# Split modulation weights in the first stage of a one-layer diffusion kernel

## The chip, the cores and the metric

The kernel runs on one core of a Trainium2 chip. It computes one layer of a hybrid diffusion backbone in float32. The metric is the device time of one execution in microseconds. Three runs of the kernel before gave 1940.58, 1941.0 and 1943.64 us, with a median of 1941.0.

The core has a matrix engine (TensorE, PE in the profile; its weight loads are shown apart as PEld), three engines for elementwise work (VectorE as DVE, ScalarE as ACT, GpSimd as POOL), and SyncE (SP), from whose queue the loads and stores are issued.

## The reference, cut to what matters

The layer modulates its normalised input with a shift and a scale that come from a conditioning vector. There are two such vectors: `c` for the latent tokens and `c_ctx` for the context tokens. The change touches the first two of six modulation parts only.

```python
mod = jax.nn.silu(c) @ w_mod[l] + b_mod[l]                       # (1, 6*1024)
mod_c = jax.nn.silu(c_ctx)[None, :] @ w_mod[l] + b_mod[l]
sh1, sc1, g1, sh2, sc2, g2 = jnp.split(mod, 6, axis=-1)
sh1c, sc1c, g1c, sh2c, sc2c, g2c = jnp.split(mod_c, 6, axis=-1)
h = modulate(rms_norm(x, norm1_w[l]), sh1, sc1)                  # latents, 1024 tokens
hc = modulate(rms_norm(ctx, norm1_w[l]), sh1c, sc1c)             # context, 256 tokens
```

with `modulate(h, shift, scale) = h * (1 + scale) + shift`. Everything after it (an input projection, attention over a window and the context, a chunked recurrence in two directions, a merge, a gated feed-forward part) is the same in both kernels.

## The kernel before

Arrays of 1024 channels are held as eight tiles of 128 partitions, and `KT` is 8. Most large products are made from split operands: a float32 value is written as a high part rounded to the type `F32R` and a low part, the rest, also in that type. TensorE multiplies such operands in one pass. Three products (high by high, high by low, low by high) stand in for one of full float32 precision; that is `mm3` at L86 to L93. The helper `split_from` (L47 to L49) makes a split: ACT copies the source into the high part (L44), and DVE subtracts the high part from the source into the low part (L49).

The first stage is `stage_startup` (L273 on). It loads the vectors, turns them on TensorE into `vecT` (L289, L290), and applies silu to both conditioning vectors, which gives `sil`, 128 partitions by 8 tiles by 2 vectors (L292). Then come two halves `i`, each with eight tiles `k` of modulation weights of 128 x 1024 floats, 512 KB each (L357 to L365). For each tile there are two products of 512 columns (L363). They are plain float32, the stationary operand is `sil[:, k]` with its two columns, and they accumulate into the two banks `pm[i]`. Of the sums only two rows are used, one for each vector. `modulation(i)` copies these rows out of both banks, one by DVE (L322) and one by ACT, turns them by eight transposes against an identity (`pmT`, L326) so that channels lie on partitions, and makes shift and scale from them with six small DVE operations (L330 to L332, tile `mods`). After the first half, the two context blocks are normalised (`norm`, L305 to L313), turned (`xct`, L348) and modulated for the first four channel tiles (`hfc` at L337 on ACT, then a split into `hcH` and `hcL`). After the second half the other four follow.

Weight tiles, token blocks and the raw context weights share one pool of eleven buffers of 128 x 1024 (`block`, tag `x`). A load into a buffer waits until the reader of what was in it is done. The loads are issued from SP's queue in program order. Split weights of the whole stage are kept in the pools of `Weights` (L53), with five buffers for high and five for low parts.

After the modulation, the stage makes the context keys (`pkc`) and values (`pvc`), the other context projections (`cx`), and the modulated latents (`xt`, `hf`, `hH`, `hL`), interleaved. The order on each engine is made by a list scheduler when the program is built, from the order in the source and its own estimates. Where `issue_after` is given, an operation is held behind another one. Each engine runs its own list strictly in order, apart from weight loads on TensorE.

Of the kernel before, what the change touches and what calls it, by code (L numbers as in the profile page):

```python
# [8 lines left out]
F32 = mybir.dt.float32  # L9
F32R = mybir.dt.float32r  # L10
AF = mybir.ActivationFunctionType
ALU = mybir.AluOpType
# [4 lines left out]
P = 128  # L17
D = 1024
# [3 lines left out]
KT = D // P  # L22
# [11 lines left out]
NFC = DFF // P  # L34
EPS = 1e-6
NEG = -1e30


class Ctx:
# [3 lines left out]
def copy_act(nc, out, in_, scale=1.0):  # L43
    return nc.scalar.activation(out, in_, AF.Copy, scale=scale)  # L44


def split_from(nc, hi, lo, src, eng="v"):  # L47
    h = copy_act(nc, hi, src)
    (nc.vector if eng == "v" else nc.gpsimd).tensor_tensor(lo, src, hi.bitcast(F32), op=ALU.subtract)  # L49
    return h  # L50
# [222 lines left out]
def stage_startup(E, at):  # L273
    nc, tc, A, ident, expo, vecT, mods = E.nc, E.tc, E.A, E.ident, E.expo, E.vecT, E.mods
    mm_tile, tp_tile, s_tile, wts = E.mm_tile, E.tp_tile, E.s_tile, E.wts
    H = KT // 2
    with ExitStack() as st:
        sp = st.enter_context(tc.tile_pool(name="st1", bufs=1, reuse_waits="tile"))
        wp = st.enter_context(tc.tile_pool(name="stw", bufs=2, reuse_waits="tile"))
        xp = st.enter_context(tc.tile_pool(name="stx", bufs=11, reuse_waits="tile"))  # L280

        def block(name):
            return xp.tile([P, D], F32, tag="x", name=name)
# [4 lines left out]
        for a in range(2):  # L288
            nc.tensor.transpose(pv[:, a * P : (a + 1) * P], rows[:, a], ident)  # L289
        nc.vector.tensor_copy(vecT, pv[:, :256])  # L290
        sil = E.sil3
        nc.scalar.activation(  # L292
            sil.rearrange("p k c -> p c k"), vecT[:, 0:16].rearrange("p (c k) -> p c k", c=2), AF.Silu
        )

        ss = sp.tile([P, NBLK], F32, name="ss")
        rs = sp.tile([P, NBLK], F32, name="rs")
# [5 lines left out]
            return t  # L303

        def norm(i, t, late=None):  # L305
            junk = wp.tile([P, D], F32, tag="junk", name=f"xj{i}", bufs=1)
            with ExitStack() as pin:
                if late is not None:
                    pin.enter_context(tc.issue_after(late.ins))
                nc.scalar.activation(junk, t, AF.Square, accum_out=ss[:, i : i + 1])  # L310
            nc.gpsimd.tensor_scalar(ss[:, i : i + 1], ss[:, i : i + 1], 1.0 / D, EPS, op0=ALU.mult, op1=ALU.add)
# [5 lines left out]
        pm = [[pm0[:2, 0:512], pm0[:2, 512:1024]], [mm_tile("pm2")[:2], mm_tile("pm3")[:2]]]  # L317
        bT = vecT[:, 32:48].rearrange("p (s k) -> p s k", s=2)

        def modulation(i):  # L320
            mrow = sp.tile([P, 1024], F32, name=f"mrow{i}", tag="mrow")[:2]
            nc.vector.tensor_copy(mrow[:, 0:512], pm[i][0])  # L322
            copy_act(nc, mrow[:, 512:1024], pm[i][1])
            pT = tp_tile(f"pmT{i}")
            for j in range(8):
                nc.tensor.transpose(pT[:, 2 * j : 2 * j + 2], mrow[:, j * P : (j + 1) * P], ident[:2, :2])  # L326
            pTv = pT[:, :16].rearrange("p (s k c) -> p s c k", s=2, c=2)
            ks = slice(H * i, H * i + H)
            for c in (1, 0):
                nc.vector.tensor_tensor(mods[:, 2 + c, ks], pTv[:, 0, c], bT[:, 0, ks], op=ALU.add)  # L330
                nc.vector.scalar_tensor_tensor(mods[:, c, ks], pTv[:, 1, c], 1.0, bT[:, 1, ks], op0=ALU.add, op1=ALU.add)
                nc.vector.tensor_tensor(mods[:, c, ks], mods[:, c, ks], vecT[:, 16 + H * i : 16 + H * i + H], op=ALU.mult)  # L332
# [25 lines left out]
        for i in range(2):  # L358
            for k in range(KT):
                w = block(f"wm{i}_{k}")  # L360
                nc.sync.dma_start(w, A["w_modA"][i][:, k])
                for n in range(2):
                    nc.tensor.matmul(  # L363
                        pm[i][n], sil[:, k], w[:, n * 512 : (n + 1) * 512], start=k == 0, stop=k == KT - 1
                    )  # L365
# [12 lines left out]
        for k2 in (2, 3):  # L378
            context(k2, pts[k2 - 2])

# [78 lines left out]
        for i in range(4):  # L459
# [222 lines left out]
def stage_mlstm(E, st):  # L682
# [96 lines left out]
    def gate_math():  # L779
        with ExitStack() as s2:  # L780
# [1068 lines left out]
def host_arrays(inp):  # L1849
# [81 lines left out]
```

## Time and profile before

| what | value |
|---|---|
| runs | 1940.58, 1941.0, 1943.64 us; median 1941.0 |
| profiled execution | span 1937.4 us from the first to the last instruction; its own time isn't given apart from the span |
| TensorE busy | 1903.1 us, 98% of the span |
| VectorE, ScalarE, GpSimd busy | 1442.4, 1000.5, 332.0 us |
| both modulation products in the chain | 15.57 us from 5.81 and 13.82 us from 23.22 |
| second half's modulated context starts | 39.21 us |

All times in the profile are microseconds from the span's start, in one execution. The chain that ended last is followed back from the last instruction, at each step to what released it. In a timeline row the first number is the start, the second the time taken, and the bracket at the end is the idle time of that engine before it and what ended it. In a group by form, the numbers are the busy time and the mean of one in ns, and then the idle time before.

### The profile page before, as it was taken

How to read it: one execution, taken by the hardware profiler on the slowest of the kernel's cores; microseconds unless marked ns; L12 is line 12 of the kernel's file. 1: busy time of each engine (PE TensorE's matmuls, PEld its weight loads, DVE VectorE, ACT ScalarE, POOL GpSimd, SP SyncE). 2: the span in 40 equal slices, each digit the busy share in tenths (PEclk: the TensorE clock that was granted, in tenths of full speed). 3: DMA queues.
4: the chain of work that ended last, by engine and by line, in shares of the span. 5: the costliest groups of instructions: out<-in, count | busy, mean ns of one | idle time of the engine just before them, and what ended most of it. 6: DMA issues, size and time to landing. Idle time of an engine off the chain costs nothing.

```text
span 1937.4 us, 28767 instructions
## 1 busy us (share of the span) xinstructions
PE 1903.1 (98%) x10012; PEld 1631.2 (84%) x10012; DVE 1442.4 (74%) x2886; ACT 1000.5 (52%) x1979; POOL 332.0 (17%) x534
## 2 busy tenths in 40 slices
PE   8999999999999999999999999999999999999999
PEld 3998888888888889999999888788888888888887
DVE  2867878777777666666657878669989898897564
ACT  4845656555556445353536556256545444455441
POOL 1323433433333132131311012010000000000000
PEclk9999999999999999999999999999999999999999
DMA  8731222313222323425235982722354534499841
GB/s 320 231 126 51 80 66 67 95 42 102 60 67 77 125 89 104 144 94 192 88 106 210 376 300 89 279 94 77 141 199 182 195 152 177 160 327 341 307 165 65
DMA packets 139377, 298.53 MB, mean 154 GB/s; under 512 B 15440, under 2 KB 39648, under 8 KB 136416
## 3 DMA queue, kind: packets, MB, share of 16 engines
q1 hardware_dynamic: 124832, 270.48, 40.3%
q10 hardware_dynamic: 14400, 26.22, 4.0%
q8 instruction: 78, 1.28, 0.3%
q14 instruction: 67, 0.55, 0.1%
HBM read 220.55 MB, written 76.10 MB: 153 GB/s over the span
## 4 chain that ended last, share of the span: by engine, by line
PE 83%; DVE 5%; DMA 4%; ACT 4%; issue 2%; POOL 1%; POOLq 0%; ACTq 0%; SPq 0%; DVEq 0%
PE pa L1513 4%; PE pa L1515 4%; PE pa L1514 4%; PE pt L625 3%; PE g L93 3%; PE g L92 3%; PE g L91 3%; PE yb L1515 2%; PE yb L1514 2%; PE yb L1513 2%; PE dx L1515 2%; PE dx L1513 2%; PE dx L1514 2%; PE pb L1513 2%; PE pb L1515 2%
## 5 line engine op out<-in xcount | busy, mean ns | idle before, releaser
L606 POOL TENSOR_SCALAR P<-P,st 128x640 f32<-128x640 f32 (+1 forms) x128 | 115.1, 916 | 261.0 <-DVE st L604 178.3
L597 ACT ACTIVATE P<-P,st 128x640 f32<-128x640 f32 (+1 forms) x128 | 102.6, 801 | 24.6 <-DVE st L593 24.0
L593 DVE CUSTOM_DVE_ANT_0 P<-s,maskA,nsink 128x640 f32<-128x640 f32 (+1 forms) x112 | 103.2, 921 | 9.4 <-PE s L590 7.8
L49 DVE TENSOR_TENSOR pl<-pt,ph 128x512 fp32r<-128x512 f32 x152 | 100.8, 686 | 10.1 <-ACT ph L44 8.6
L44 ACT ACTIVATE ph<-pt 128x512 fp32r<-128x512 f32 x152 | 87.4, 597 | 36.9 <-PE pt L625 32.5
L91 PE MATMUL g<-hH,fh 128*128 128x512 f32 x256 | 102.7, 401 | 0.0
L93 PE MATMUL g<-hH,fl 128*128 128x512 f32 x256 | 100.6, 393 | 0.0
L92 PE MATMUL g<-hL,fh 128*128 128x512 f32 x256 | 100.6, 393 | 0.0
L625 PE MATMUL pt<-ident,P 128*128 128x128 f32 x608 | 92.3, 273 | 3.5 <-POOL P L606 3.1
L91 PE MATMUL pq<-w1h,hH 128*128 128x384 f32 (+1 forms) x256 | 87.1, 340 | 0.2 <-DVE t L545 0.2
L91 PE MATMUL kv<-w1h,hH 128*128 128x384 f32 x256 | 86.5, 339 | 0.8 <-ACT w1h L44 0.8
L93 PE MATMUL pq<-w1h,hL 128*128 128x384 f32 (+1 forms) x256 | 86.7, 339 | 0.0
L92 PE MATMUL kv<-w1l,hH 128*128 128x384 f32 x256 | 86.6, 338 | 0.0
L92 PE MATMUL pq<-w1l,hH 128*128 128x384 f32 (+1 forms) x256 | 86.5, 338 | 0.0
L93 PE MATMUL kv<-w1h,hL 128*128 128x384 f32 x256 | 86.3, 337 | 0.0
L625 PEld LDWEIGHTS pt<-ident,P 128*128 128x128 f32 x608 | 71.1, 140 | 11.5 <-POOL P L606 6.4
L91 PE MATMUL mo<-w1h,hH 128*128 128x256 f32 x256 | 72.6, 284 | 0.4 <-ACT sg L774 0.2
L93 PE MATMUL mo<-w1h,hL 128*128 128x256 f32 x256 | 72.1, 282 | 0.0
L92 PE MATMUL mo<-w1l,hH 128*128 128x256 f32 x256 | 71.9, 281 | 0.0
L1651 ACT ACTIVATE cv<-ua,vecT 128x1024 f32<-128x1024 f32 x22 | 27.4, 1245 | 83.6 <-DVE ua L1624 83.6
L929 POOL TENSOR_SCALAR kwh<-k,gcall 128x128 fp32r<-128x128 f32 x72 | 32.7, 457 | 215.8 <-PE dC L92 112.1
L1513 PE MATMUL dx<-dwh,dfh 128*128 128x512 f32 x176 | 68.7, 390 | 0.0
(587 smaller groups left out, 6392.9 us busy)
## 6 DMA issues: line engine op xcount, KB each, us to landing
ur<-in_w_up SPq DMA_DIRECT2D x22, 1024.0 KB, 4.9
wmb<-in_w_modB SPq DMA_DIRECT2D x48, 256.0 KB, 2.9
f_d<-cv SPq DMA_DIRECT2D x22, 512.0 KB, 2.6
wm<-in_w_modA SPq DMA_DIRECT2D x16, 512.0 KB, 9.2
fr<-in_w_g SPq DMA_DIRECT2D x32, 256.0 KB, 3.1
drf<-fs_d SPq DMA_DIRECT2D x15, 512.0 KB, 6.8
drw<-wt_d SPq DMA_DIRECT2D x14, 512.0 KB, 6.0
w1b<-in_w_cx SPq DMA_DIRECT2D x16, 388.0 KB, 4.0
```

The source lines that it names most:

```text
L44: return nc.scalar.activation(out, in_, AF.Copy, scale=scale)
L49: (nc.vector if eng == "v" else nc.gpsimd).tensor_tensor(lo, src, hi.bitcast(F32), op=ALU.subtract)
L91: nc.tensor.matmul(ps, lh[:, ls], rh[:, rs], start=start and i == 0, stop=False)
L92: nc.tensor.matmul(ps, lh[:, ls], rl[:, rs], start=False, stop=False)
L93: nc.tensor.matmul(ps, ll[:, ls], rh[:, rs], start=False, stop=stop and i == n - 1)
L593: nc.vector.tensor_tensor_reduce(pm[:, :W], ps[:, off : off + W], mask[:, :W], scale=ss[:, h : h + 1], scalar=nsink[:, hh : hh + 1], op0=A ...
L597: nc.scalar.activation(pm[:, :W], pm[:, :W], AF.Exp, bias=st4[:, h : h + 1], scale=-1.0, accum_out=st4[:, 4 + h : 5 + h])
L606: nc.gpsimd.tensor_scalar(Ps[h][:, :W], Ps[h][:, :W], st4[:, 12 + h : 13 + h], 1.0, op0=ALU.mult, op1=ALU.mult)
L625: nc.tensor.transpose(pt[:, h * P : (h + 1) * P], Ps[h][:, kb * P : (kb + 1) * P], ident)
L1513: nc.tensor.matmul(ps, lh, rh, start=start and i == 0, stop=False, skip_group_check=True)
L1514: nc.tensor.matmul(ps, lh, rl, start=False, stop=False, skip_group_check=True)
L1515: nc.tensor.matmul(ps, ll, rh, start=False, stop=stop and i == n - 1, skip_group_check=True)
```

## The change

Of the eight weight tiles of each half, six (all but tiles 2 and 5, `WHOLE`) are now split into a high and a low part with `split_from`, into a pool of their own with two buffers for each part. The stationary operand for these is a new constant `sp4`: for each tile 100 columns (`MS`), of which columns 0 and 1 hold the high parts of the two vectors, columns 2 and 3 their low parts, and the rest zeros. So a product with the high and one with the low part of the weights, each for two banks, gives four rows: rows 0 and 1 belong to the high parts of the vectors and rows 2 and 3 to the low ones. They are made in one pass each, and with four partial products, where `mm3` has three. Tiles 2 and 5 keep the plain float32 products into rows 0 and 1 of the same banks.

The four rows must be added in pairs. This is done in the turning: the eight transposes are replaced by eight float32 products of the four rows with a 4 x 2 matrix `sel` of ones and zeros, which adds row 0 to row 2 and row 1 to row 3.

`sp4` takes one of the five high buffers of `Weights` until the second half's products are done. The pool `stw` of the later part of the stage is opened only after `modulation(1)`, in the place of the split tiles, and the tile `junk` of `norm` moves to another pool for it.

```diff
+MS = 100
+WHOLE = (2, 5)
@@ stage_startup
-        wp = st.enter_context(tc.tile_pool(name="stw", bufs=2, reuse_waits="tile"))
         xp = st.enter_context(tc.tile_pool(name="stx", bufs=11, reuse_waits="tile"))
+        sm = ExitStack()
+        md = sm.enter_context(tc.tile_pool(name="stm", bufs=2, reuse_waits="tile"))
...
+        sp4 = wts.hp.tile([P, 2, 400], F32R, tag="h", name="sp4").rearrange("p a b -> p (a b)").rearrange("p (k m) -> p k m", m=MS)
+        nc.gpsimd.memset(sp4.bitcast(F32), 0.0)
+        copy_act(nc, sp4[:, :, 0:2], sil)
+        nc.vector.tensor_tensor(sp4[:, :, 2:4], sil, sp4[:, :, 0:2].bitcast(F32), op=ALU.subtract)
+        sel = sp.tile([P, 2], F32, name="sel")
+        nc.vector.tensor_tensor(sel[:4], ident[:4, 0:2], ident[:4, 2:4], op=ALU.add)
...
-            mrow = sp.tile([P, 1024], F32, name=f"mrow{i}", tag="mrow")[:2]
-            nc.vector.tensor_copy(mrow[:, 0:512], pm[i][0])
-            copy_act(nc, mrow[:, 512:1024], pm[i][1])
+            mrow = sp.tile([P, 1024], F32, name=f"mrow{i}", tag="mrow")[:4]
+            nc.vector.tensor_copy(mrow[:, 0:512], pm[i][0][:4])
+            copy_act(nc, mrow[:, 512:1024], pm[i][1][:4])
             pT = tp_tile(f"pmT{i}")
             for j in range(8):
-                nc.tensor.transpose(pT[:, 2 * j : 2 * j + 2], mrow[:, j * P : (j + 1) * P], ident[:2, :2])
+                nc.tensor.matmul(pT[:, 2 * j : 2 * j + 2], mrow[:, j * P : (j + 1) * P], sel[:4], start=True, stop=True)
...
-                for n in range(2):
-                    nc.tensor.matmul(
-                        pm[i][n], sil[:, k], w[:, n * 512 : (n + 1) * 512], start=k == 0, stop=k == KT - 1
-                    )
+                if k in WHOLE:
+                    for n in range(2):
+                        nc.tensor.matmul(
+                            pm[i][n][:2], sil[:, k], w[:, n * 512 : (n + 1) * 512], start=False, stop=False,
+                            skip_group_check=True,
+                        )
+                else:
+                    wh, wl = [md.tile([P, D], F32R, tag=f"m{x}", name=f"m{x}{i}_{k}") for x in "hl"]
+                    split_from(nc, wh, wl, w)
+                    for x, wx in enumerate((wh, wl)):
+                        for n in range(2):
+                            nc.tensor.matmul(
+                                pm[i][n][:MS], sp4[:, k], wx[:, n * 512 : (n + 1) * 512], start=k == 0 and x == 0,
+                                stop=k == KT - 1 and x == 1, skip_group_check=True,
+                            )
...
         modulation(1)
+        sm.close()
+        wp = st.enter_context(tc.tile_pool(name="stw", bufs=2, reuse_waits="tile"))
```

In the order as built, the new work is placed as follows. On ACT the copies of the second half's tiles 0 and 1 stand before the first context work (`hfc`, `hcH`), those of tiles 3, 4, 6 and 7 behind it. On TensorE five of the second half's products, on tiles 0 and 1, stand ahead of the first half's turning. On DVE the subtraction of the second half's tile 0 stands ahead of the first half's row copy, and a subtraction of the context key weights stands between the first and the second of the six small operations of the second half's modulation. The rest of the program has the same order in both, but for a few neighbours that change places.

More of the change, by code (lines that the diff above doesn't have):

```diff
@@ L305, in norm @@
         def norm(i, t, late=None):
-            junk = wp.tile([P, D], F32, tag="junk", name=f"xj{i}", bufs=1)
+            junk = sp.tile([P, D], F32, tag="junk", name=f"xj{i}", bufs=1)
             with ExitStack() as pin:
@@ L316, in stage_startup @@
         pm0 = s_tile("pm0")
-        pm = [[pm0[:2, 0:512], pm0[:2, 512:1024]], [mm_tile("pm2")[:2], mm_tile("pm3")[:2]]]
+        pm = [[pm0[:, 0:512], pm0[:, 512:1024]], [mm_tile("pm2"), mm_tile("pm3")]]
         bT = vecT[:, 32:48].rearrange("p (s k) -> p s k", s=2)
         def modulation(i):
-            mrow = sp.tile([P, 1024], F32, name=f"mrow{i}", tag="mrow")[:2]
-            nc.vector.tensor_copy(mrow[:, 0:512], pm[i][0])
-            copy_act(nc, mrow[:, 512:1024], pm[i][1])
+            mrow = sp.tile([P, 1024], F32, name=f"mrow{i}", tag="mrow")[:4]
+            nc.vector.tensor_copy(mrow[:, 0:512], pm[i][0][:4])
+            copy_act(nc, mrow[:, 512:1024], pm[i][1][:4])
             pT = tp_tile(f"pmT{i}")
             for j in range(8):
-                nc.tensor.transpose(pT[:, 2 * j : 2 * j + 2], mrow[:, j * P : (j + 1) * P], ident[:2, :2])
+                nc.tensor.matmul(pT[:, 2 * j : 2 * j + 2], mrow[:, j * P : (j + 1) * P], sel[:4], start=True, stop=True)
             pTv = pT[:, :16].rearrange("p (s k c) -> p s c k", s=2, c=2)
```

## The prediction

> **What bounds the kernel now.** I read the page's first part, then the chain that ended last in order of time for the first 72 us, then the timeline of each engine there.
>
> ```profile
> span 1937.4 us, 28767 instructions
> PE 1903.1 (98%) x10012; PEld 1631.2 (84%) x10012; DVE 1442.4 (74%) x2886; ACT 1000.5 (52%) x1979; POOL 332.0 (17%) x534
> ```
>
> TensorE is busy for 98% of the span. The change lies in the first 2% of it, so what matters is how early the later work can start. The chain of the first stage:
>
> ```profile
> 1.64 4.04 DMA wm<-in_w_modA
> 5.81 15.57 PE pm L363 x32
> 23.22 13.82 PE pm L363 x32
> 37.05 1.02 PE xct L348 x8
> 38.07 0.59 PE pmT L326 x8
> 39.21 1.02 ACT hfc L337 x2
> 42.36 1.05 ACT xj L310 x2
> 49.76 2.22 ACT w1h L44 x3
> 63.57 0.67 ACT hf L337
> ```
>
> The two halves of the modulation product (pm) fill the chain up to 37 us; after the turning (pmT) the chain passes to ScalarE (ACT), which holds most of it past 63 us. So the handle on the end is the start of the second half's modulated context, hfc at 39.21: what follows it stands in the same order in both programs as built (a few neighbours swap), and I let a shift of hfc reach the end one for one.
>
> The loads, from the rows of the weight tiles' line (issue times, then the time to landing) and the stretch view (PE, PEld, DVE, ACT, POOL, clock, DMA share, GB/s):
>
> ```profile
> L361 SPq DMA_DIRECT2D wm<-in_w_modA x1: 327/327/327, 9.6 to 9.6; - x1
> DMA to landing us min/median/max: 10.3/10.3/10.3
> ...
> L361 SPq DMA_DIRECT2D wm<-in_w_modA x1: 328/328/328, 18.0 to 18.0; - x1
> DMA to landing us min/median/max: 8.3/8.3/8.3
> 5.80:21.30 15.50, 15.49 (x32) 2.79 (x32) 2.19 (x3) 2.30 (x4) 1.50 (x4) 1.00 1.02 409
> ```
>
> The second tile of the second half lands at 9.6 + 10.3 = 19.9, the seventh at 18.0 + 8.3 = 26.3: one per 1.28. Counting back and forth, the first half's last tile lands at 17.4, the second half's first at 18.7 and its last at 27.6. The DMA share is full, so these landings stay.
>
> **The change part by part.** Prices first (groups by form, then timeline rows; start, time):
>
> ```profile
> L363 PE MATMUL pm<-wm,sil 128*2 128x512 f32 x64 | 29.5, 620 | 1.3 <-DMA wm<-in_w_modA 1.3
> L310 ACT ACTIVATE xj<-x 128x1024 f32<-128x1024 f32 x4 | 4.2, 1054 | 7.2 <-DMA x<-in_ctx 7.2
> L49 DVE TENSOR_TENSOR w1l<-w1b,w1h 128x776 fp32r<-128x776 f32 x16 | 15.7, 993 | 1.6 <-ACT w1h L44 1.6
> L49 DVE TENSOR_TENSOR w1l<-w1b,w1h 128x512 fp32r<-128x512 f32 x8 | 5.2, 682 | 2.2 <-ACT w1h L44 2.2
> 172.04 0.39 PE L92 MATMUL g<-hL,fh 128*128 128x512 f32 x1
> 172.27 0.39 PE L93 MATMUL g<-hH,fl 128*128 128x512 f32 x1
> 173.18 0.94 PE L221 MATMUL ms<-expo,macc 128*128 128x1 f32 x8
> ```
>
> *Products.* The 32 products show as 64 passes; 13.82 / 32 = 0.43 a pass, so a whole tile (two products) costs 1.73. A single-pass product of this width starts 0.23 after its neighbour, so a split tile (four) costs 0.92. TensorE: before 15.57 + 13.82 = 29.4; after 48 x 0.23 + 8 x 0.86 = 17.9: 11.5 less. No row has 100 stationary columns: its ends are 0.23 and the 0.86 of a two-pass product; I take 0.23, the same type and width.
>
> *Splits.* Twelve copies on ACT at 1.05 each (the square over 128x1024 is the nearest), of which 0.1 overlaps the next. Twelve subtractions on VectorE (DVE): 0.682 at 512 and 0.993 at 776 columns make an estimated 1.28 at 1024, 1.2 from start to start. Per split tile the way is copy, subtract, low products, and the engines work on neighbouring tiles together, so a tile costs no more than its landing of 1.28, as long as nothing else holds ACT or DVE.
>
> *Turning.* Eight transposes become eight fp32 products with two columns. The nearest rows on both sides are the 0.59 of today's eight and the eight passes (four instructions) of ms, 0.94 with their drain, so 16 passes are about 1.75; ms loads 128 rows of weights, these only 4. I take 1.4, nearer to ms, which is a product of the same type; ends 0.6 and 1.75.
>
> *Small ones.*
>
> ```profile
> 12.18 0.19 POOL L311 TENSOR_SCALAR ss<-ss 128x1 f32<-128x1 f32 x1 [11.35 <-ACT xj L310]
> 30.21 5.48 SPq L302 DMA_DIRECT2D x<-in_x  x4
> ```
>
> The memset of 128x800 on POOL, the copy and subtraction of 128x16, the sum of two 4x2 pieces: POOL's first other work is at 12.18; ACT and DVE do theirs beside the first tile, which makes the first product start at about 8.2 instead of 5.81. That is made good by tile three, since 0.92 is under 1.28. Cost zero, 2.4 if the products stayed behind. The constant's place is one of five high buffers: the first context-value weights take it over, needed only after the context keys, and its last use is at about 35: zero. The work pool now lies where the split tiles were, whose last use is also at about 35: zero.
>
> *First half.* Last tile: landing 17.4, copied 18.5, subtracted 19.8, products done at 20.3. In the order as built DVE now first subtracts the second half's tile 0 (copied 19.8) until 21.05, then copies the row (0.68) until 21.75. PE has five products of the second half ahead of the turning, the last on tile 1, whose ACT copy stands behind ACT's row copy (20.4 to 21.0): 22.05. So the turning starts at 22.3 and ends at 23.7. Before (timeline):
>
> ```profile
> 20.56 0.68 DVE L322 COPY mrow<-pm 2x512 f32<-2x512 f32 x1 [4.13 <-PE pm L363]
> 21.42 0.59 ACT L44 ACTIVATE mrow<-pm 2x512 f32<-2x512 f32 x1 [6.69 <-PE pm L363]
> 22.89 0.16 DVE L330 TENSOR_TENSOR mods<-pmT,vecT 128x4 f32<-128x4 f32 x1 [1.65 <-PE pmT L326]
> 23.41 1.02 ACT L337 ACTIVATE hfc<-xct,mods 128x256 f32<-128x256 f32 x2 [1.41 <-DVE mods L331]
> 25.84 0.72 ACT L44 ACTIVATE hcH<-hfc 128x256 fp32r<-128x256 f32 x2
> 38.69 0.16 DVE L330 TENSOR_TENSOR mods<-pmT,vecT 128x4 f32<-128x4 f32 x1 [0.58 <-PE pmT L326]
> ```
>
> From turning to hfc is 23.41 - 22.89 = 0.52, so hfc starts at 24.25, 0.85 later than now, although the products ended a microsecond earlier.
>
> *Second half.* The copies of its tiles 3, 4, 6 and 7 stand on ACT behind the first context work (hfc to hcH, 23.41 to 26.56 = 3.15 now), so behind 27.3, though tile 3 landed at about 22.5. Here the splits wait for what the first half made late. Copies: tile 3 to 28.35; 4 to 29.3; 6 to 30.25; 7 must wait until PE has used tile 4's high part (two buffers), at about 30.7, and ends at 31.75. Subtractions 3, 4, 6, 7 end at 29.65, 30.85, 32.05, 33.3. PE: tile 3's low part and tile 4 until 31.35, the whole tile 5 until 33.1, tiles 6 and 7 (eight products) until 34.9; drained 35.05. Before, 37.04. Then the row copy until 35.75, turning until 37.15, and one modulation operation, behind which DVE's order now has a 128x512 subtraction (0.68) before the other five: 37.2 + 0.52 + 0.65 = 38.4 for hfc, against 39.21: 0.8 earlier. Of 11.5 us saved on PE that is all that reaches ACT.
>
> *Queues.* SP's order is the same here. Each load now waits for a split where it waited for a product. The last key weights wait for the whole tile 2, used at about 27.3 and so are issued 1 earlier; the four x blocks go out from about 28 on (30.21 now). By my account ACT asks for the last key weights and the first block at about 36: zero gain on a chain that ACT holds, zero cost.
>
> **Sum.** 1937.4 - 0.8 = 1936.6. The profiled execution's own time isn't shown apart from its span; the runs are 1940.58, 1941.0 and 1943.64, median 1941.0, or 3.6 above the span. So 1941.0 - 0.8 = 1940.2. With the turning at 1.75 both halves lose 0.35: 1940.9. At 0.6 both gain 0.8: 1938.6.
>
> A rule that speaks against the change: the Trainium skill, page "TensorE: Matmul & The Clock Gate", section Terms, calls the transpose mode 4x faster for FP32, and the turning gives it up. By that the eight would cost about 2.4 by estimate, both halves lose 1.0 more and the time would be 1942.2. The ms rows speak for less, as their cost is in passes and weight loads, not in columns.
>
> **Rivals.** *Faster: ACT's order does not bind.* If the last landing alone set the end, it would go 27.6 + 1.05 + 1.28 + 0.46 of products + 0.15 + 0.68 + 1.4 + 0.52 = 33.1 for hfc, 6.1 earlier: 1934.9. For it speaks that loads and buffers come free earlier. Against it, the order as built. It needs a gain further down of 3 on top of mine to pass 3.9.
>
> *Slower: PE's clock.* Weight loads of the first products (start, time):
>
> ```profile
> 7.47 0.13 PEld L363 LDWEIGHTS pm<-wm,sil 128*2 128x2 f32 x1 [0.73 <-issue]
> 8.32 0.13 PEld L363 LDWEIGHTS pm<-wm,sil 128*2 128x2 f32 x1 [0.73 <-issue]
> 9.63 0.09 PEld L363 LDWEIGHTS pm<-wm,sil 128*2 128x2 f32 x1 [0.34 <-issue]
> 10.06 0.09 PEld L363 LDWEIGHTS pm<-wm,sil 128*2 128x2 f32 x1 [0.34 <-issue]
> ```
>
> Passes are 0.85 apart until about 9.2 and 0.43 after, that is, half speed for the first 3.4 us of products. Now PE runs without a pause; after, it is busy about 0.9 of each 1.28 and 0.5 of each 1.2 around 29. If it falls back, an episode of 3.4 at half speed loses 1.7. One: 1941.9. Two: 1943.6. From the third on (end of the first half, second half, first context products) it is slower by over 0.2%: 1945.3. Against it:
>
> ```profile
> 66.40 0.65 PE L454 MATMUL kct<-ident,kkc 128*128 128x128 f32 x4 [1.05 <-ACT kkc L44]
> 68.06 0.63 PE L454 MATMUL kct<-ident,klc 128*128 128x128 f32 x4 [1.01 <-DVE klc L391]
> 69.49 0.34 PE L92 MATMUL cx<-w1l,hcH 128*128 128x388 f32 x1
> 69.67 0.34 PE L93 MATMUL cx<-w1h,hcL 128*128 128x388 f32 x1
> ```
>
> Two gaps of a microsecond leave the next products 0.18 apart, full speed. The Trainium skill, same page, Part 1, has the clock fall after an idle window of about 3.4 us; no gap of my account is that long, so by it this rival fails; these rows agree as far as they go, but show no thin work for 15 us.
>
> *It does not do what it says.* If products with 100 columns ran in two passes (0.86), PE would need 56 x 0.86 = 48 instead of 29.4, up to 18.8 slower: 1959. No row with this operand type does.
>
> **Numbers.** Forecast (the chain through ACT) 0.58, its own range 1938.2 to 1942.3; faster rival 0.2; clock 0.19; two passes 0.03. A measurement of this kernel can tell about 0.2%, 3.9 us, from no change. The forecast, and one or two episodes of the clock (0.02), are within it: 0.6; faster 0.2; slower 0.2. The range leaves about half of each outer case out: 1935.8 to 1945.5.
>
> **What would show it.** In the changed profile: hfc of the first half at about 24.2 (over 25: turning too cheap here), ACT's copy of tile 3 right behind hcH, the second half's products done at about 35, hfc of the second half at 38.4, pmT at 1.4. Landings unchanged. The forecast is wrong if passes of 0.43 for single-pass products appear after 20 us, if hfc's shift is not found again at the first attention products, or if the copies run ahead of the context work.

## The result and the profile after

The changed kernel takes 1947.76 us (median of 18 runs), the kernel before 1942.39 us (18 runs beside them). The ratio is 1.0028, with a 95% interval of 1.002 to 1.0036. One of the 18 runs of each kernel (2670.95 and 10759.3 us) was in a far slower state and is left out of the ratio and of everything below. So the change is slower by 0.28%, where 1940.2 us and no measurable change were forecast. The profiled execution took 1952.47 us, with a span of 1950.7 us.

Here is the chain that ended last, of the changed kernel (start, duration):

```profile
22.43 2.22 PE pmT L337 x16
...
27.83 3.21 PE pm L375 x4
...
35.73 2.04 PE pm L384 x8
...
38.82 1.87 PE pmT L337 x16
```

Two things stand out. The turning (pmT) is 16 passes and takes 1.9 to 2.2 us, where eight transposes took 0.59. And the same line L375 (a whole tile's two products) takes 3.21 us here and 1.81 us further down in the same trace: TensorE runs at half speed there. The stretch view of the changed kernel shows where else (its columns: stretch and length, then PE, PEld, DVE, ACT, POOL, granted clock, DMA share, GB/s):

```profile
23.80:30.60 6.80, 6.80 (x20) 3.44 (x19) 2.92 (x11) 4.86 (x10) 0.00 (x0) 0.50 0.77 290
40.90:44.20 3.30, 3.30 (x17) 3.30 (x17) 2.57 (x9) 2.39 (x6) 0.00 (x0) 0.50 0.99 360
71.60:75.00 3.40, 3.35 (x13) 3.38 (x14) 3.39 (x4) 2.15 (x4) 1.70 (x3) 0.50 0.14 56
747.50:750.80 3.30, 3.30 (x17) 3.30 (x17) 2.27 (x12) 2.46 (x8) 2.37 (x9) 0.50 0.00 0
846.50:853.20 6.70, 5.95 (x28) 5.95 (x28) 4.93 (x22) 3.25 (x10) 3.14 (x13) 0.50 0.00 0
948.90:952.20 3.30, 3.30 (x17) 3.30 (x17) 2.88 (x11) 2.79 (x10) 0.61 (x2) 0.50 0.00 0
```

The granted clock is 0.50 in all six. Each is one or two units of 3.41 us, so that is eight units. The trace of before has one of them after its start (next view). This comparison of two traces overstates the difference: the traced execution of the change is the slowest of the runs kept, and that of before has a mean granted clock of 0.999, where the runs of the kernel before average 0.9973 to 0.9975 in the table further down.

```profile
934.30:937.60 3.30, 2.79 (x13) 2.79 (x14) 2.75 (x14) 1.24 (x4) 1.90 (x8) 0.50 0.00 0
```

The other lines that answer to those of the prediction, from the timeline of the changed kernel (start, duration, and in the bracket the idle time before):

```profile
19.24 0.63 PE L384 MATMUL pm<-mh,sp 128*100 128x512 f32 x2
19.70 0.63 PE L384 MATMUL pm<-ml,sp 128*100 128x512 f32 x2
22.36 2.29 PE L337 MATMUL pmT<-sel,mrow 4*128 4x2 f32 x16
25.74 1.02 ACT L348 ACTIVATE hfc<-xct,mods 128x256 f32<-128x256 f32 x2 [3.84 <-PE xct L359]
28.77 2.00 ACT L48 ACTIVATE mh<-wm 128x1024 fp32r<-128x1024 f32 x2
37.14 0.63 PE L384 MATMUL pm<-ml,sp 128*100 128x512 f32 x2
38.75 1.94 PE L337 MATMUL pmT<-sel,mrow 4*128 4x2 f32 x16
41.81 1.02 ACT L348 ACTIVATE hfc<-xct,mods 128x256 f32<-128x256 f32 x2 [1.86 <-DVE mods L343]
```

The single-pass products start 0.23 us apart, and ACT's copies do stand behind the first context work. The second half's products end at 37.8, and its context work (hfc) starts at 41.81, which is 2.6 us later than the 39.21 of before and not 0.8 earlier. Further down the delay grows: one product that both kernels have (tile dC) starts at 737.91 in the trace of before and at 746.76 here, 8.85 later, and the spans differ by 13.3. Its row before, and then its row after:

```profile
737.91 0.36 PE L91 MATMUL dC<-VH,kwh 128*128 128x258 f32 x1 [1.87 <-DVE C L937]
```

```profile
746.76 0.36 PE L95 MATMUL dC<-VH,kwh 128*128 128x258 f32 x1 [1.87 <-DVE C L961]
```

### The profile page after: what moved, and what is told of

Read it like the earlier page. It is cut to its first block, busy times and chain, and to the rows that moved or that the text cites. A ratio compares the mean times of both kernels' runs of the same rounds, so it can differ in the third digit from the quotient of the medians.

```text
span 1950.7 us, 28850 instructions
## 1 busy us (share of the span) xinstructions
PE 1908.7 (98%) x10028; PEld 1646.8 (84%) x10028; DVE 1455.4 (75%) x2900; ACT 1012.5 (52%) x1992; POOL 331.4 (17%) x535
## 3 DMA queue, kind: packets, MB, share of 16 engines
q8 instruction: 79, 1.29, 0.3%
## 4 chain that ended last, share of the span: by engine, by line
PE 79%; DVE 7%; DMA 6%; ACT 5%; issue 2%; POOL 1%; POOLq 0%; SPq 0%; ACTq 0%; DVEq 0%
PE pa L1537 4%; PE pa L1538 4%; PE pa L1539 4%; PE g L97 3%; PE pt L649 3%; PE g L96 3%; PE g L95 3%; PE dx L1539 2%; PE dx L1537 2%; PE dx L1538 2%; PE po L643 2%; PE pb L1538 2%; PE pb L1539 2%; PE pb L1537 2%; PE kv L95 2%
```

## The experiments

The theories were three: the turning's price, TensorE's clock, and the place of the second half's work ahead of the first turning. Each result stands beside runs of the kernel before on the same chip. Every run lists its span and its mean granted clock, so the loss can be divided. Over the 229 runs of this study, with an offset of its own for each kernel, a run is 1.6 us longer for each 0.001 by which its mean clock is lower. That slope times the difference of the mean clocks is called "by the clock" below, and what is left "the rest". The division rests on a correlation over runs; a unit of 3.41 us at half speed lowers the mean by 0.0009 and can cost 1.7 us at most, which agrees with it.

The traces show the cost of one unit directly, at a place where all kernels run the same code. The rows of VectorE and ScalarE can be matched one by one with those of the trace of before, and their delay taken at 60 to 66 us and at 72 to 76 us (medians, by the time in before). In the ten traces that have a half-speed unit at about 66 to 72 us the delay grows by 1.6 to 1.8 us between the two; in the three that have none there (before again, first half only, added rows again) it grows by 0.1.

In the table, the times in the last column contain half-speed stretches of their own traces for placed, 64 columns and one pass.

| kernel | ratio, 95% interval | mean span against before, us | mean clock, this and before | by the clock | rest | hfc of second half in its trace (39.21 before) |
|---|---|---|---|---|---|---|
| the change again | 1.0029, 1.0019 to 1.0038 | +5.7 | 0.9950, 0.9973 | +3.7 | +2.0 | 40.26 |
| turning alone | 1.0032, 1.0021 to 1.0044 | +5.8 | 0.9970, 0.9975 | +0.8 | +5.0 | 42.02 |
| splits with transposes | 0.9995, 0.9985 to 1.0006 | -1.0 | 0.9971, 0.9975 | +0.6 | -1.6 | 37.56 |
| filled | 1.0029, 1.0018 to 1.0040 | +5.2 | 0.9963, 0.9975 | +2.0 | +3.2 | 41.08 |
| first half only | 1.0007, 0.9997 to 1.0017 | +1.6 | 0.9974, 0.9975 | +0.1 | +1.5 | 41.09 |
| added rows | 0.9986, 0.9978 to 0.9995 | -2.5 | 0.9971, 0.9973 | +0.3 | -2.9 | 37.05 |
| placed | 1.0019, 1.0009 to 1.0029 | +4.4 | 0.9958, 0.9973 | +2.4 | +2.0 | 41.30 |
| both edits | 0.9994, 0.9985 to 1.0003 | -1.3 | 0.9966, 0.9973 | +1.1 | -2.4 | 36.78 |
| 64 columns | 1.0016, 1.0006 to 1.0026 | +3.1 | 0.9963, 0.9974 | +1.7 | +1.4 | 39.48 |
| one pass | 1.0001, 0.9991 to 1.0011 | +0.1 | 0.9964, 0.9974 | +1.6 | -1.6 | 38.94 |
| added rows again | 0.9984, 0.9975 to 0.9994 | -3.3 | 0.9973, 0.9974 | +0.2 | -3.4 | 37.02 |

**The turning alone.** The kernel before, with products in place of its transposes; TensorE keeps its full float32 products.

```diff
-                nc.tensor.transpose(pT[:, 2 * j : 2 * j + 2], mrow[:, j * P : (j + 1) * P], ident[:2, :2])
+                nc.tensor.matmul(pT[:, 2 * j : 2 * j + 2], mrow[:, j * P : (j + 1) * P], ident[:2, :2], start=True, stop=True)
```

> The kernel before with one part of the change alone: the eight transposes of each turning are products with a 2 x 2 identity in plain float32. If the turning is what costs (theory T), each turning takes about 1.9 us instead of 0.6 to 0.7, hfc of the second half starts 1.3 to 2.5 us later than 39.21 and the time is 1 to 2.5 us above the kernel before. If the clock is what costs (theory C), TensorE stays as dense as before, no half-speed window shows in the first 45 us, and apart from the turning itself nothing is lost: under 1.5 us. Both theories have the turning's own price in common; the run sizes it.

```profile
21.54 1.05 PE L326 MATMUL pmT<-ident,mrow 2*128 2x2 f32 x8
39.52 1.94 PE L326 MATMUL pmT<-ident,mrow 2*128 2x2 f32 x16
42.02 1.03 ACT L337 ACTIVATE hfc<-xct,mods 128x256 f32<-128x256 f32 x2 [1.79 <-DVE mods L331]
```

The timeline of this kernel shows 16 passes at full clock as 1.94 us, against 0.59 for the eight transposes: 1.35 more per half, and hfc of the second half starts 2.8 later. The turning alone makes the kernel slower by 0.32%, as much as the whole change. Its loss is larger than the shift at hfc by 2.2 us, and larger than the 1 to 2.5 us that were expected; I could not place all of it. In its trace the delay grows from 2.8 to 4.5 us across a half-speed unit at 70.8 us, which neither trace of before has.

**The splits with transposes.** The change, with eight transposes of rows 0 and 1 in place of the products; what the low parts of the two vectors add (rows 2 and 3) is left out.

```diff
-                nc.tensor.matmul(pT[:, 2 * j : 2 * j + 2], mrow[:, j * P : (j + 1) * P], sel[:4], start=True, stop=True)
+                nc.tensor.transpose(pT[:, 2 * j : 2 * j + 2], mrow[:2, j * P : (j + 1) * P], ident[:2, :2])
```

> The changed kernel with the transposes put back. The rows of the vectors' low parts are left out of the result, so the rows are not added; all products, copies and subtractions of the splits stay. Theory T: hfc of the second half moves from 41.81 back by about 2.5 us to 39.3, and the time falls by 2 to 3 us below the changed kernel. Theory C: TensorE is at least as thin, the half-speed windows between 20 and 45 us stay, and the time stays within 1.3 us of the changed kernel.

```profile
35.80 0.65 PE L337 MATMUL pmT<-ident,mrow 2*128 2x2 f32 x8
37.56 1.02 ACT L348 ACTIVATE hfc<-xct,mods 128x256 f32<-128x256 f32 x2 [0.57 <-DVE mods L343]
```

The splits by themselves bring hfc of the second half 1.65 us forward, to 37.56 where 39.3 was expected, but the interval of the ratio holds 1. No half-speed stretch stands between its start and 45 us, though TensorE's work is as thin there; its trace has two later, at 66 and 933 us.

**Filled.** The change, with eight useless single-pass products into an unused bank at the end of each half, so that TensorE has more to do ahead of the turning.

```diff
+        scratch = E.fl_tile("fill")
+        def fill(i, wx, count):
+            for j in range(count):
+                nc.tensor.matmul(scratch[:MS], sp4[:, 0], wx[:, j % 2 * 512 : (j % 2 + 1) * 512], start=True, stop=True, skip_group_check=True)
...
+            fill(i, wh, 8)
```

> The changed kernel with eight single-pass products into an unused bank added at the end of each half (1.9 us of TensorE work each), in time in which TensorE waits. Theory C: the windows before the two turnings are dense enough, no half-speed window shows from 15 to 45 us, hfc of the second half starts at 39 to 40 in place of 41.81, and the time is 1.5 to 3 us below the changed kernel. Theory T or placement (the second half's work ahead of the first turning): hfc stays at 41 or later, and the time is equal to the changed kernel or up to 1 us above.

Its trace has no half-speed stretch between its start and 70 us, but both turnings still cost 1.94 us and stand behind the fill, and hfc comes 1.9 late. Later stretches stay (70, 743, 842 and 941 us). So with more work on TensorE the first stage's stretches are absent from this one trace, but the time does not get better, because that work takes its own.

**The first half only.** Only the first half is split and turned by products; the second is as before.

```diff
-                if k in WHOLE:
+                if i == 1 or k in WHOLE:
...
+                if i == 0:
+                    nc.tensor.matmul(pT[:, 2 * j : 2 * j + 2], mrow[:, j * P : (j + 1) * P], sel[:4], start=True, stop=True)
+                else:
+                    nc.tensor.transpose(pT[:, 2 * j : 2 * j + 2], mrow[:, j * P : (j + 1) * P], ident[:2, :2])
```

> The change in the first half alone: six of its eight tiles are split and its turning is the product; the second half has its sixteen plain products and transposes. Theory C: the second half's products are dense, so no half-speed window shows after 24 us, and the time is within 1.5 us of the kernel before. Theory T: one turning at 1.9 us, hfc of the second half 0 to 1.3 us later than 39.21. If the splits as such (ACT and DVE time) are what costs, the first half's hfc starts at 25 or later and the time is 2 us or more above the kernel before.

hfc comes 1.9 late, more than the expected 1.3, as dense float32 products follow a late first turning (hfc of its first half starts at 26.42, against 23.41 before). There is no stretch between its start and 100 us, but its trace has five units from 742 us on. Its mean clock over the runs is that of the kernel before, its loss of 1.6 us is nearly all rest, and the interval of the ratio holds 1.

**The change again.** Unaltered, for a second trace and its clocks beside the next three.

> The change itself, unaltered, beside the three variants below. Three theories share its loss. Turning: the product form costs 1.3 us more than the transposes in each half. Clock: TensorE's granted clock falls during the thin work of the first 45 us, and later at a phase that depends on the run. Placement: second-half work stands ahead of the first half's turning. All of them expect a ratio near 1.003 and hfc of the second half at 40 to 42 us; by the clock theory that start is 40 to 40.5 in an execution that has no half-speed stretch between 20 and 45 us, and 41.5 to 42 in one that has.

This trace holds what the first could not show, both turnings at full clock:

```profile
22.55 1.94 PE L337 MATMUL pmT<-sel,mrow 4*128 4x2 f32 x16
25.12 1.02 ACT L348 ACTIVATE hfc<-xct,mods 128x256 f32<-128x256 f32 x2 [3.03 <-PE xct L359]
35.59 0.62 PE L384 MATMUL pm<-ml,sp 128*100 128x512 f32 x2
37.20 1.94 PE L337 MATMUL pmT<-sel,mrow 4*128 4x2 f32 x16
40.26 1.02 ACT L348 ACTIVATE hfc<-xct,mods 128x256 f32<-128x256 f32 x2 [1.86 <-DVE mods L343]
```

With the clock full up to the end of the second turning, hfc is 1.05 late; in the first trace it was 2.6 late, so the stretch at 23.80 to 30.60 cost about 1.55 there. A stretch of 3.4 us follows from 39.6 on, and the later ones stand within about a microsecond of where the first trace has them (here at 70, 746, 845 and 948 us). This execution, too, is near the slow end of its runs (1951.29 of 1945.21 to 1951.89 us).

**Added rows.** The change, but four rows are turned by transposes, and the low pair is added by two small operations on VectorE.

```diff
-                nc.tensor.matmul(pT[:, 2 * j : 2 * j + 2], mrow[:, j * P : (j + 1) * P], sel[:4], start=True, stop=True)
-            pTv = pT[:, :16].rearrange("p (s k c) -> p s c k", s=2, c=2)
+                nc.tensor.transpose(pT[:, 4 * j : 4 * j + 4], mrow[:, j * P : (j + 1) * P], ident[:4, :4])
+            pT4 = pT[:, :32].rearrange("p (j r c) -> p j r c", r=2, c=2)
+            low = sp.tile([P, 8, 2], F32, name=f"low{i}", tag="low")
+            nc.vector.tensor_copy(low, pT4[:, :, 1])
+            pS = sp.tile([P, 16], F32, name=f"pS{i}", tag="pS")
+            nc.vector.tensor_tensor(pS.rearrange("p (j c) -> p j c", c=2), pT4[:, :, 0], low, op=ALU.add)
+            pTv = pS.rearrange("p (s k c) -> p s c k", s=2, c=2)
```

> The change, but the four rows are turned by eight transposes into 32 columns, and the low pair is added to the high pair by two small VectorE operations (a copy and a sum of 128x16). Turning theory: the eight transposes take 0.65 us instead of 1.94, the two operations 0.3 to 0.5, so each half wins 0.8 to 1.0 us, hfc of the second half starts at 38 to 38.6 us and the time is 2 us or more below the change again, within 0.1% of the kernel before. Clock theory alone: the transposes leave TensorE as thin as in the change, the half-speed stretches stay and the time is within 1 us of the change again.

```profile
23.52 0.17 DVE L340 COPY low<-pmT 128x16 f32<-128x16 f32 x1
23.72 0.17 DVE L342 TENSOR_TENSOR pS<-pmT,low 128x16 f32<-128x16 f32 x1
34.97 0.66 PE L337 MATMUL pmT<-ident,mrow 4*128 4x4 f32 x8 [0.54 <-DVE mrow L333]
37.05 1.02 ACT L353 ACTIVATE hfc<-xct,mods 128x256 f32<-128x256 f32 x2 [0.43 <-DVE mods L348]
```

Transposes of four rows cost what those of two did, the two operations 0.41 together. hfc is 2.16 earlier than before the change (37.05, where 38 to 38.6 was expected), and the kernel is faster than the one before by 0.14%. The mean clock goes back from 0.9950 to 0.9971. The clock theory taken alone expected the stretches to stay; those of the first 45 us did not, while three single units stand later in this trace (67, 739 and 937 us).

**Placed.** The change with its product turning, but the second half's subtractions are held behind the first half's last modulation operation, and its products behind the first turning.

```diff
+                E.turn = nc.tensor.matmul(pT[:, 2 * j : 2 * j + 2], mrow[:, j * P : (j + 1) * P], sel[:4], start=True, stop=True)
+                E.mod = nc.vector.tensor_tensor(mods[:, c, ks], mods[:, c, ks], vecT[:, 16 + H * i : 16 + H * i + H], op=ALU.mult)
...
+                    with ExitStack() as pin:
+                        if i == 1:
+                            pin.enter_context(tc.issue_after(E.mod.ins))
+                        split_from(nc, wh, wl, w)
...
+                            if i == 1:
+                                pin.enter_context(tc.issue_after(E.turn.ins))
```

> The change with the product form of the turning, but the second half's subtractions are held behind the first half's last modulation operation on VectorE, and the second half's products behind the first half's turning on TensorE. Placement theory: the first turning starts 1 to 1.5 us earlier (21 to 21.4 us at full speed), hfc of the first half at about 24 instead of 25.7, and 1 to 1.5 us of it reach hfc of the second half, so the time is 1 to 1.5 us below the change again. Turning theory: the two product turnings stay at 1.94 us each, so it remains 2 to 3 us over the variant with both edits. If the second half is bound by its own splits, held later, hfc of the second half is not earlier and the time is the same or longer.

```profile
21.33 2.27 PE L337 MATMUL pmT<-sel,mrow 4*128 4x2 f32 x16 [0.77 <-DVE mrow L333]
41.30 1.02 ACT L348 ACTIVATE hfc<-xct,mods 128x256 f32<-128x256 f32 x2 [0.73 <-DVE mods L343]
```

The turning does start 1.2 us earlier. The mean span is 1.3 us below that of the change again, as the placement theory expected, but the intervals of the two ratios overlap, and by the division all of it goes with the clock: the rest is 2.0 as in the change. A double stretch of half speed stands in this trace's first stage too, so its hfc can't decide this.

**Both edits.** Added rows and the placement.

> Both edits together: transposes and added rows, and the second half's subtractions and products held behind the first half's end. Turning and placement theories: hfc of the first half at 22.8 to 23.4 us, of the second at 36.8 to 37.6 (39.21 in the kernel before), and a time 1.5 to 2.4 us below the kernel before, a ratio of 0.9988 to 0.9992. Clock theory alone: half-speed stretches between 20 and 45 us stay and the ratio is 1.002 or more.

```profile
22.70 1.02 ACT L353 ACTIVATE hfc<-xct,mods 128x256 f32<-128x256 f32 x2 [0.86 <-DVE mods L348]
31.37 0.71 PE L398 MATMUL pm<-mh,sp 128*100 128x512 f32 x2
32.83 0.63 PE L398 MATMUL pm<-ml,sp 128*100 128x512 f32 x2
36.78 1.02 ACT L353 ACTIVATE hfc<-xct,mods 128x256 f32<-128x256 f32 x2 [0.61 <-DVE mods L348]
```

hfc of the first half comes 1.8 earlier than with added rows alone, that of the second only 0.27, and the time is no better. The second half's products now run one behind the other up to 33.5 (first and last row of the last two tiles). So beside transposes the placement was worth next to nothing.

**64 columns.** The change, with 64 columns in the moving operand of each turning product, 62 of them zeros.

```diff
-        sel = sp.tile([P, 2], F32, name="sel")
+        sel = sp.tile([P, 64], F32, name="sel")
+        nc.gpsimd.memset(sel, 0.0)
...
-                nc.tensor.matmul(pT[:, 2 * j : 2 * j + 2], mrow[:, j * P : (j + 1) * P], sel[:4], start=True, stop=True)
+                nc.tensor.matmul(pT[:, 64 * j : 64 * j + 64], mrow[:, j * P : (j + 1) * P], sel[:4], start=True, stop=True)
```

> The change with 64 columns in each turning product instead of two (the other 62 are zeros and are not read). If the price of the turning goes by its 16 passes, pmT stays at 1.9 to 2.1 us and hfc of the second half at 40.3 us (41.8 with a half-speed stretch before it), as in the change. If it goes by columns, pmT grows to well over 3 us. Clock theory in the form that passes of two columns count as idle: with 64 columns no half-speed stretch stands between 20 and 45 us, the mean clock rises from 0.995 to 0.996 or more and the ratio falls to 1.001 to 1.002; in the form that any thin work counts, the stretches and the ratio of 1.003 stay.

```profile
36.98 1.99 PE L338 MATMUL pmT<-sel,mrow 4*128 4x64 f32 x16 [0.53 <-DVE mrow L334]
36.85 1.46 DVE L53 TENSOR_TENSOR w1l<-w1b,w1h 128x512 fp32r<-128x512 f32 x2
39.48 1.02 ACT L349 ACTIVATE hfc<-xct,mods 128x256 f32<-128x256 f32 x2 [0.85 <-DVE mods L344]
```

32 times the columns cost 0.05 us: the price is in the passes, and not in their columns. The subtraction of key weights (w1l) now stands ahead of the six modulation operations and not between them, which is why hfc is earlier than in the change. The mean clock (0.9963) and the ratio (1.0016) are where the first form of the clock theory put them, but a half-speed unit stayed in its first stage (at 24.5 us), which that form excluded. So neither form is borne out by this run.

**One pass.** Rows and selector rounded to the single-pass type, so eight passes; what the rounding cuts off each row is left out.

```diff
-        sel = sp.tile([P, 2], F32, name="sel")
+        sel = sp.tile([P, 2], F32R, name="sel")
-            mrow = sp.tile([P, 1024], F32, name=f"mrow{i}", tag="mrow")[:4]
+            mrow = sp.tile([P, 1024], F32R, name=f"mrow{i}", tag="mrow")[:4]
```

> The change with rows and selector of the turning rounded to the single-pass type: eight passes instead of sixteen. The part of each row below that rounding is left out. If the price goes by passes, pmT takes 0.9 to 1.1 us instead of 1.94, each half wins 0.9 us, hfc of the second half starts at 38.3 to 38.8 us and the clock-free loss of 1.9 us against the kernel before turns to about zero; with the clock as in the change the ratio is 1.001 to 1.002, with the clock as in the kernel before 0.9995 to 1.0005. If the price goes by the type or the weight loads alone, pmT stays over 1.5 us.

```profile
36.78 1.05 PE L337 MATMUL pmT<-sel,mrow 4*128 4x2 f32 x8
38.94 1.02 ACT L348 ACTIVATE hfc<-xct,mods 128x256 f32<-128x256 f32 x2 [0.97 <-DVE mods L343]
```

Half the passes, half the price (1.05, as each group of eight passes in the first experiment). The expectation took this run to tell passes from weight loads, which it does not: each pass has a weight load of its own, so there are eight loads here and 16 in the change, in both 0.11 us from start to start, where those of the transposes are 0.06 apart. The loss against the kernel before goes, though its mean clock stays low and two stretches stand in its first stage.

**Added rows again, and the kernel before again.** Both unaltered. The first is a second reading of the faster variant, the second another trace of the kernel before (a single run, 1939.37 us).

> The variant with eight transposes and added rows once more, on whatever chip comes: hfc of the second half at 36.9 to 37.2 us, 2.0 to 2.3 us earlier than in the kernel before, and a ratio of 0.998 to 0.9995 if the gain holds; within 0.9995 to 1.0005 if the earlier reading was chance.

> The kernel before, unaltered, for a second trace of it: hfc of the second half again at 39.1 to 39.3 us, no half-speed stretch between 20 and 60 us. If the change alone provokes the later stretches (at about 70, 745, 845 and 945 us in its traces), this trace has none before 900 us, as the first one of this kernel. If they belong to waits that both kernels have and come or not with the phase, some of them stand here too, at places some 9 us earlier from 735 us on.

The gain held: 0.9984, interval 0.9975 to 0.9994. The second trace of the kernel before (stretch view, columns as above) is full up to 930 us and has its one stretch where the first trace had it:

```profile
14.00:45.00 31.00, 31.00 (x133) 12.90 (x131) 10.27 (x30) 13.79 (x30) 2.22 (x6) 1.00 0.93 339
...
934.00:938.00 4.00, 2.80 (x14) 2.60 (x13) 3.45 (x13) 1.48 (x4) 2.90 (x9) 0.63 0.00 0
```

So places late in the program can repeat. They need not: of the units of added rows at 67, 739 and 937 us, the trace of added rows again has the last two (736 and 934) and not the first. The same stretch view for 14 to 45 us has a granted clock of 1.00 in the four traces with thin products and transposes (splits with transposes, added rows twice, both edits), in those with dense products (before, turning alone), and in the filled and the first-half kernels. It is below 1.00 in all five traces with thin products in both halves and product turnings: 0.83 and 0.94 for the change, 0.89 placed, 0.94 with 64 columns, 0.89 with one pass. Here the two ends of that comparison, the changed kernel and then added rows:

```profile
14.00:45.00 31.00, 29.78 (x127) 18.27 (x126) 19.34 (x36) 19.09 (x35) 1.48 (x4) 0.83 0.89 337
```

```profile
14.00:45.00 31.00, 27.92 (x148) 16.81 (x147) 23.03 (x46) 23.84 (x43) 3.74 (x8) 1.00 0.91 347
```

## Why the prediction was wrong, point by point

Two steps of the sum failed. The turning was taken at 1.4 us and measured 1.94. And the sum held nothing for TensorE's clock, because a rival that priced it was argued down from two gaps of a microsecond; over runs, 3.7 of the 5.7 us lost go with the clock.

- **Products and splits: right.** Single-pass products with 100 columns cost 0.23 each, the subtraction 1.23 (estimated 1.28), the copy 1.06, and the first product started at 8.01 (8.2). The two-pass rival fell. The splits alone brought hfc of the second half 1.65 us forward.
- **Turning: mis-sized.** The sum took 1.4 us between ends of 0.6 and 1.75; it measured 1.94, above the upper end. That end came from eight passes in 0.94 minus shared drain; eight passes are 1.05, and 16 are 1.94. The columns (two or 64) do not matter, the number of passes, each with its weight load, does. The transposes I counted 1.4 against are 0.65. The Trainium skill, page "TensorE: Matmul & The Clock Gate", section Terms, has 4x, or about 2.4 us here by estimate; the rows show 3x, so the measured time lies between my value and that of the rule.
- **First half: right in form, late by 0.87.** At full clock (the change again) hfc started at 25.12, where 24.25 was forecast: 0.54 of the turning, 0.25 of its later start, the rest at the context turning. My mark of "over 25: turning too cheap" was the right reading.
- **Second half: the carry was right.** The copies did stand behind the first context work, and the lateness went through to the products, which ended at 36.2 instead of 35.05. Behind them the order has a context product ahead of the turning, which I had not listed: the turning's chain time is 37.27 where the row copy alone would have let it start before 37. With the second turning's 0.54, 38.4 became 40.26. What the first half lost reached the second, but what it wins does not go further: with both edits hfc of the second half moves 0.27 for 1.8, so once nothing is carried the second half is bound by its own products, which stand one behind the other there.
- **The handle: only roughly right.** I let a shift of hfc reach the end one for one. In the table the rest lies within 1.5 us of the shift of hfc, but for the turning alone, where it is 2.2 more. That is more than the 0.8 us that was forecast.
- **The clock: put at nothing, and the larger loss.** The rival had a chance of 0.19 and said that from the third episode on the kernel is slower by over 0.2%. Over runs the mean clock falls from 0.9973 to 0.9950, which is between two and three more units of 3.41 us, and 3.7 of the 5.7 us go with it. I argued the rival away with gaps of a microsecond that left the clock full. The Trainium skill, same page, Part 1, has the clock fall after an idle window of 3.4 us. That a unit is 3.41 us and that stretches are whole units of it agrees. That it takes an idle window does not, if idle is what the profile shows as idle: between 16.42 and 23.80 in the changed kernel's trace TensorE had no gap over 0.54 us and still fell to half. I had also looked for it in the first stage only; the units at 70, 747, 846 and 948 us lie in stages which the change does not touch, so the rival was right in its price for a unit and only in part about the place.
- **What goes ahead of a fall.** The traces' rows show more than gaps do. Cut each of the fourteen traces into windows of 3.41 us that end where the clock can change, and count the moving columns of the passes that start in a window (those of the plain float32 weight products twice, as they take 0.43 us where others take 0.23). For the window ahead of the first fall in the changed kernel's trace, 20.39 to 23.80, these are the rows, with the turning at 22.36 shown above:

```profile
20.17 0.63 PE L384 MATMUL pm<-mh,sp 128*100 128x512 f32 x2
21.34 0.71 PE L384 MATMUL pm<-ml,sp 128*100 128x512 f32 x2 [0.54 <-DVE ml L53]
21.95 0.48 PE L384 MATMUL pm<-mh,sp 128*100 128x512 f32 x1
```

Four of these products start in the window (2,048 columns), and 13 passes of the turning (26 columns): 2,074 in all. Of the 50 windows ahead of a half-speed unit 47 hold at most 3,100 columns, and of the 7,832 other windows 16 do. Between 14 and 45 us the windows ahead of a unit hold 800 to 2,576 columns, and each holds all or part of a product turning, whose 16 passes occupy TensorE for 1.94 us with 32 columns in the change. In the four traces with thin products and transposes, which take 0.65 us, no window there holds under 3,104.

So the sum, -0.8 forecast against +5.7 in the change again, splits into about 1.1 for the two turnings, 0.75 for what else was late in the two halves, 0.9 between hfc and the end, and 3.7 by the clock. That the form of the turning is what makes the change slower is shown by the turning alone, one pass, and added rows. The 3.7 rest on the correlation over runs, on the 1.6 to 1.8 us that one unit costs, and on the kernels with transposes, in which clock and time came back together. Thin products with product turnings lose the clock in the first stage because, by the count above, they leave too few columns in a window; this is read off the traces and was not tested by a run that changes the columns alone. Why the later units come more often with them stays open. The phase plays a part: ahead of the unit at 747 us in the changed kernel the window holds 2,824 columns, and the wait of 1.87 us that ends at 746.76 lies wholly within it, while in before the window that holds most of the same wait (from 736.25) has 3,604 and the clock stays full.

## What to carry to other kernels

Price a tiny TensorE operation by its passes, not by its columns: a turning by float32 products costs three times that of transposes, and two added elementwise operations (0.41 us together) were cheaper than the 1.29 us that the products cost more in each half. Before making a dense TensorE stage thinner, price the clock as well, and count columns and not busy time: an operation that keeps TensorE busy with two columns a pass looks dense in the profile, and the clock fell behind it here. When a change wins on one half and loses on a small step at its end, replace that step alone: here this turned 0.28% slower into 0.15% faster.

## What the runs showed of the hardware

- The granted clock changes only in whole units of 3.41 us. Some late places repeat from one trace of a program to the next (934 and 935 us in the two of before; 70 to 72, 746 to 748, 845 to 847 and 948 to 949 us in the two of the change), others come in one trace only (23.80 in the change, 67 in added rows). It fell without any TensorE gap over 0.54 us.
- A unit at half speed at about 66 to 72 us costs 1.6 to 1.8 us in ten traces, and the delay grows by 0.1 there in three traces without it.
- In fourteen traces, 47 of 50 half-speed units follow a window of 3.41 us with at most 3,100 moving columns, and 16 of 7,832 other windows hold as few. Some records of products can be missing, so the line is not sharp.
- A float32 product of 4 rows by 128 columns of weights and two moving columns shows as two passes of 0.12 us, each with its weight load; with 64 moving columns it takes the same. A transpose of the same piece takes 0.08 (0.65 for eight), with two rows or four.
- The mean granted clock of a run explains much of the scatter between runs of one kernel: 1.6 us per 0.001 over 229 runs.
